# The first FFN unit of a streaming-encoder block, written out in a fixed order with half weight tiles, and the second half of the norm's sum moved among the second unit's products

## The chip, the core and the metric

The kernel runs on one NeuronCore of a Trainium2 chip. The metric is device time in microseconds (us) of one execution, median of several runs. Five engines run their own instruction queues side by side: TensorE (PE: matrix products and transposes, with PEld for its weight loads), VectorE (DVE), ScalarE (ACT), GpSimd (POOL) and SyncE (SP, which here issues most of the transfers from memory). An instruction that waits for another engine holds up everything behind it in its own queue.

## The reference

One layer on a sequence of 512 tokens of width 1024, float32:

```
x = x + 1/2 * SwiGLU(RMSNorm(x))        # FFN 1, inner width 2816
h = RMSNorm(x); p = h @ W_in            # then two token mixers, RWKV-7 and forgetting attention
x = x + (sigmoid(g_A) * y_A + sigmoid(g_B) * y_B) @ W_out
x = x + 1/2 * SwiGLU(RMSNorm(x))        # FFN 2
out = RMSNorm(x)
# SwiGLU(h) = (silu(h @ w1) * (h @ w3)) @ w2
# RMSNorm(x) = x * rsqrt(mean(x*x) + 1e-6) * gain
```

Everything in this document happens in the first lines of FFN 1: loading x, its norm, and the first columns of `h @ w1` and `h @ w3`.

## The kernel before

**Layout.** x is kept transposed, as eight tiles `xT[0..7]` of 128 features x 512 tokens. x arrives in four quarters `xin0..3` (128 x 4 x 256, 512 KB each). PE transposes each quarter into two tiles in PSUM (`xtp`, four transposes a tile), and ACT copies them out to `xT`.

**Float32 products from two parts.** Each operand is split into a high part (rounded to the matrix format) and a low part (the rest): `xh`/`xl` for x times the norm's gain, `firsth`/`firstl` or `whi`/`wlo` for weights. One product of x and w is then three matrix products: high by high, high by low, low by high (`mm3`, lines L130 to L132). The norm's division comes later: products run on x times gain, and the result is multiplied by `rstd` when it leaves PSUM.

**FFN 1** goes in 22 units of 128 columns of w1 and w3. A unit is 2 x 8 x 3 = 48 products of 128x512, one PSUM bank for w1's columns (`f0` in the first unit, `pa` later) and one for w3's (`f1`, `pb`). Its weights come as two tiles of 128x8x128 (512 KB); ACT casts the high part (L122), DVE subtracts for the low part (L123). The loop for units 1 to 21 (second unit on) is in `ffn`; the first unit is written out ahead of it, among the transposes.

**The first unit before.** The transfers go on SP's queue in the order xin0, w1's tile, xin1, w3's tile, xin2, xin3. For each of the eight tiles of x: transposes, copy, high part (on ACT or DVE, by turns), low part on DVE (L182 to L185), then the products whose inputs are there. The order in which the instructions finally stand on each engine is set by a scheduler, which places them by its own estimate of readiness; `tc.keep_in_program_order` pins an instruction at the place where it is written, and `tc.issue_after(i)` puts an instruction behind `i` if both are on the same engine (it makes no engine wait for another). The low part of w3's first tile is cut by POOL.

**The norm.** `nrm.square` squares each tile of x on ACT and adds the squares up (`acc`, the first two additions on POOL, the others on DVE). `nrm.gather` makes the last addition and splits the sum into two halves `shi` (ACT) and `slo` (DVE). `nrm.sums` adds over the 128 partitions on PE, by two products with a matrix of ones (`ssum`, L148): they stand among the products of the second unit. `nrm.root` makes `rstd` of it (ACT); then `evacuate` can empty the first unit's two banks (`fa`, `fb` ...).

**Warm products.** Eight products of a matrix of ones (`warm`, L242) run on PE at the start, before x is there; their result is not used.

Of the kernel before, what the change touches and what calls it, by code (L numbers as in the profile page):

```python
# [18 lines left out]
P = 128  # L19
# [32 lines left out]
def kernel(  # L52
# [73 lines left out]
    def load_w(aps, kt, n, eng=None, own=None):  # L126
        return split_w(load_raw(aps, kt, n), kt, n, eng, own)
# [17 lines left out]

    def summed(ps, mat, parts):
        for i, part in enumerate(parts):
            pe.matmul(ps, mat[:], part[:], start=i == 0, stop=i == 1)  # L148

    def exact(ps, mat, src):  # L150
        summed(ps, mat, halved(src))
# [17 lines left out]
    class Norm:  # L169
# [39 lines left out]

        def sums(s):  # L210
            s.ps = bank("ssum", pr)
            summed(s.ps[:], onesr, s.parts)

        def root(s):
            ln = tmp("rln")
# [29 lines left out]
    dve.tensor_copy(par[:, 0:8], gtp[:, 0:8])  # L245
    nrm = Norm(PAR_FFN1)
    with tc.tile_pool(name="x0", bufs=1) as x0:
        xin = [x0.tile([P, NB, D // 4], F32, name=f"xin{g}") for g in range(4)]
        own = [[x0.tile([P, KD, P], F32R, name=f"first{i}{w}") for i in "hl"] for w in range(2)]
        wraw = [x0.tile([P, KD, P], F32, name=f"wraw{w}") for w in range(2)]  # L250
        first = []
        for g in range(4):
            nc.sync.dma_start(xin[g][:], x[0, :, g * 256:(g + 1) * 256].rearrange("(b p) c -> p b c", p=P))
            for w, at in ((ffn1_w1, 0), (ffn1_w3, 1)):
                if g == at:
                    first.append(load_raw([(0, w[0][:, 0:P])], KD, P, wraw[at]))
        for c in range(KD):
            ps = bank("xtp", pr)
            for b in range(NB):
                pe.transpose(ps[:, b * P:(b + 1) * P], xin[c // 2][:, b, (c % 2) * P:(c % 2 + 1) * P], ident[:])  # L260
            cx = act.copy(xT[c][:], ps[:])
# [4 lines left out]
            for i, at in enumerate((0, 2)):  # L266
                for k in range(KD):
                    if c == max(k, at) if k <= at else c == k:
                        ps, (wh, wl) = first[i]
                        mm3(ps[:], wh[:, k, :], wl[:, k, :], nrm.hi[k][:], nrm.lo[k][:], k == 0, k == KD - 1)  # L270
# [67 lines left out]
    def ffn(nrm, w1, w3, w2, nxt, during=(), first=None, final=None):  # L338
        with tc.tile_pool(name="hp", bufs=1) as hp:
            hh, hl, done = [], [], []  # L340

            def evacuate():
                while done:
                    j, pa, pb = done.pop(0)
                    a = tmp("fa")
                    dve.tensor_tensor(a[:], pa[:], nrm.rstd[:], op=ALU.mult)  # L346
# [12 lines left out]
            for j in range(KF):  # L359
                c0 = j * P  # L360
                early = j == 1 and first
                if j == 0 and first:
                    pa, pb = [f[0] for f in first]
# [707 lines left out]
```

## Time and profile before

| what | before |
|---|---|
| median of 3 runs | 1191.12 us (1190.68 to 1191.21) |
| the profiled execution | 1190.24 us, its span 1188.5 us |
| PE busy | 1169.2 us (98%) |
| DVE / ACT / POOL busy | 662.1 / 457.1 / 100.4 us |
| moved by transfers | 122.54 MB, mean 103 GB/s |
| first product of the second unit (`pa`) | 24.80 us after the span's start |

The span is the time between the first and the last instruction of the profile; the execution's own time has 1.7 us more around it. Busy time of an engine is the sum over its instructions; one engine's idle time costs nothing as long as another carries the end. The granted clock of PE (1.00 is full speed) is given by stretches.

### The profile page before, as it was taken

The page shows a single profiled execution, that of the slowest core. Times are in us where ns is not written, and L with a number is a line of the kernel's source. Part 1 is how long each engine was busy: PE and PEld are TensorE (multiplying, and loading weights), DVE is VectorE, ACT ScalarE, POOL GpSimd, SP SyncE. Part 2 cuts the span into 40 slices and gives each one's busy share as a digit, 9 for nine tenths or more (in the row PEclk, how much of TensorE's full clock was granted, in tenths as well). Part 3 has the DMA queues.
Part 4 walks back from the last instruction along what each step waited for, and adds up shares of the span by engine and source line. Part 5 has one row for each costly group of instructions (what it writes and reads, how often), then busy time and mean ns, then how long its engine had stood idle before and what let it go on. Part 6 is the DMA issues. An engine that isn't in the chain of part 4 may idle for free.

```text
span 1188.5 us, 15870 instructions
## 1 busy us (share of the span) xinstructions
PE 1169.2 (98%) x6334; PEld 952.3 (80%) x6334; DVE 662.1 (56%) x993; ACT 457.1 (38%) x739; POOL 100.4 (8%) x144
## 2 busy tenths in 40 slices
PE   8999999999999999999999999999999999999997
PEld 7888888888887888887767777778888888888887
DVE  6555545443444888686766657866545545543242
ACT  6322222222223855346776756524222222222221
POOL 4200000001111112401000011121000000000110
PEclk9999999999999999999999999999999999999999
DMA  7333333323333433344212135633333333323331
GB/s 200 89 91 104 89 106 89 103 83 115 116 116 96 121 108 111 111 124 116 55 46 87 55 99 175 193 100 107 89 98 98 90 105 91 104 80 98 98 98 72
DMA packets 208152, 122.54 MB, mean 103 GB/s; under 512 B 9902, under 2 KB 200430, under 8 KB 208078
## 3 DMA queue, kind: packets, MB, share of 16 engines
q1 hardware_dynamic: 202078, 108.67, 31.8%
q0 software_dynamic: 3760, 12.06, 3.2%
q8 instruction: 50, 0.82, 0.3%
q10 hardware_dynamic: 2240, 0.79, 0.3%
q14 instruction: 24, 0.20, 0.1%
HBM read 110.82 MB, written 10.68 MB: 102 GB/s over the span
## 4 chain that ended last, share of the span: by engine, by line
PE 95%; DVE 3%; ACT 1%; DMA 1%; issue 0%; POOL 0%; SPq 0%; DVEq 0%; POOLq 0%
PE pd L131 7%; PE pd L130 7%; PE pd L132 7%; PE pa L132 7%; PE pa L131 7%; PE pb L131 7%; PE pb L132 7%; PE pa L130 7%; PE pb L130 7%; PE pgt L130 3%; PE pgt L132 2%; PE pgt L131 2%; PE pk L130 2%; PE pk L132 2%; PE pk L131 2%; PE pw L132 1%
## 5 line engine op out<-in xcount | busy, mean ns | idle before, releaser
L122 ACT CAST whi<-raw 128x1024 fp32r<-128x1024 f32 (+2 forms) x197 | 196.4, 998 | 605.9 <-PE pa L131 175.5
L123 DVE TENSOR_TENSOR wlo<-raw,whi 128x1024 fp32r<-128x1024 f32 (+2 forms) x197 | 227.5, 1155 | 129.1 <-ACT whi L122 129.0
L132 PE MATMUL pa<-xh,wlo 128*128 128x512 f32 x344 | 133.9, 389 | 0.0
L131 PE MATMUL pa<-xl,whi 128*128 128x512 f32 x344 | 133.8, 389 | 0.0
L132 PE MATMUL pb<-xh,wlo 128*128 128x512 f32 x344 | 133.8, 389 | 0.0
L130 PE MATMUL pa<-xh,whi 128*128 128x512 f32 x344 | 133.8, 389 | 0.0
L130 PE MATMUL pb<-xh,whi 128*128 128x512 f32 x344 | 133.8, 389 | 0.0
L131 PE MATMUL pb<-xl,whi 128*128 128x512 f32 x344 | 133.8, 389 | 0.0
L132 PE MATMUL pd<-hh,wlo 128*128 128x512 f32 x330 | 129.0, 391 | 0.0
L131 PE MATMUL pd<-hl,whi 128*128 128x512 f32 x330 | 128.5, 389 | 0.0
L130 PE MATMUL pd<-hh,whi 128*128 128x512 f32 x330 | 128.4, 389 | 0.0
L350 DVE TENSOR_TENSOR fb<-pb,rstd 128x512 f32<-128x512 f32 x43 | 29.7, 691 | 137.2 <-PE pb L132 137.2
L130 PEld LDWEIGHTS pa<-xh,whi 128*128 128x128 f32 x344 | 64.6, 188 | 13.5
L132 PEld LDWEIGHTS pb<-xh,wlo 128*128 128x128 f32 x344 | 64.6, 188 | 13.4
L131 PEld LDWEIGHTS pb<-xl,whi 128*128 128x128 f32 x344 | 64.6, 188 | 13.5
L132 PEld LDWEIGHTS pa<-xh,wlo 128*128 128x128 f32 x344 | 64.5, 188 | 13.5
L131 PEld LDWEIGHTS pa<-xl,whi 128*128 128x128 f32 x344 | 64.6, 188 | 13.4
L130 PEld LDWEIGHTS pb<-xh,whi 128*128 128x128 f32 x344 | 64.5, 188 | 13.4
L131 PEld LDWEIGHTS pd<-hl,whi 128*128 128x128 f32 x330 | 61.9, 188 | 12.9
L132 PEld LDWEIGHTS pd<-hh,wlo 128*128 128x128 f32 x330 | 62.0, 188 | 12.7
L130 PEld LDWEIGHTS pd<-hh,whi 128*128 128x128 f32 x330 | 62.0, 188 | 12.7
L346 DVE TENSOR_TENSOR fa<-pa,rstd 128x512 f32<-128x512 f32 x43 | 29.7, 691 | 68.5 <-PE pa L132 68.4
(397 smaller groups left out, 1964.5 us busy)
## 6 DMA issues: line engine op xcount, KB each, us to landing
raw<-in_ffn_w_dram SPq DMA_DIRECT2D x116, 512.0 KB
raw<-in_w_in_dram SPq DMA_DIRECT2D x40, 512.0 KB
raw<-in_ffn_w_dram SPq DMA_DIRECT2D x15, 384.0 KB
raw<-in_w_out_dram SPq DMA_DIRECT2D x8, 512.0 KB
gsave<-gs SPq DMA_DIRECT2D x9, 256.0 KB
xin<-in_x_dram SPq DMA_DIRECT2D x4, 512.0 KB
xsave<-xT POOLq DMA_DIRECT2D x8, 256.0 KB, 2.3
G<-gsave POOLq DMA_DIRECT2D x8, 256.0 KB, 3.8
```

Source lines behind the costliest of these rows:

```text
L122: act.copy(hi[:], raw[:])
L123: (eng or dve).tensor_tensor(lo[:], raw[:], hi[:].bitcast(F32), op=ALU.subtract)
L130: pe.matmul(ps, whi, xhi, start=first, stop=False)
L131: pe.matmul(ps, whi, xlo, start=False, stop=False)
L132: return pe.matmul(ps, wlo, xhi, start=False, stop=last)
L346: dve.tensor_tensor(a[:], pa[:], nrm.rstd[:], op=ALU.mult)
L350: dve.tensor_tensor(b[:], pb[:], nrm.rstd[:], op=ALU.mult)
```

## The change

The first unit is written out by hand, every instruction pinned in its place (`keep`):

- The weights of the first unit come as four half tiles of 128x4x128 (256 KB each): `w0`, `w1` are the two halves of w1's columns, `w2`, `w3` those of w3's. The transfers' order is x0, w0, x1, w1, x2, x3, w2, w3. Each half has its own cast (`cut(i, False)`, ACT) and subtraction (`cut(i, True)`, DVE).
- Four more warm products follow the transposes of x's first quarter.
- PE makes all products of w1's columns first, each as soon as its tile of x is meant to be ready, with the transposes between them, and then those of w3's; the products of the last tile with w1 stand behind half of w3's.
- ACT makes the high parts of tiles 1, 3, 5, 7, DVE those of 0, 2, 4, 6 and all low parts; POOL has nothing to do in the first unit. All additions of squares are on DVE, behind the last subtraction, and the squares on ACT behind the last cast; the second unit's weights are cut behind these too.
- The second product of the norm's sum (`slo`) stands behind two groups of three products of the second unit's `pb`; before, the scheduler had it further back.

The core of the diff (`turn(c)`: four transposes of tile c; `copy(c)`: `xT[c]` on ACT; `cut(i, lo)`: high or low part of weight half i; `part(c, lo)`: high or low part of tile c of x; `product(w, k, n)`: the n-th of the three products of bank `f0` or `f1` with tile k; the last part is in `ffn`, where `early` is the second unit):

```diff
-        for g in range(4):
-            nc.sync.dma_start(xin[g][:], x[0, :, g * 256:(g + 1) * 256].rearrange("(b p) c -> p b c", p=P))
-            for w, at in ((ffn1_w1, 0), (ffn1_w3, 1)):
-                if g == at:
-                    first.append(load_raw([(0, w[0][:, 0:P])], KD, P, wraw[at]))
-        for c in range(KD):
-            ps = bank("xtp", pr)
-            for b in range(NB):
-                pe.transpose(ps[:, b * P:(b + 1) * P], xin[c // 2][:, b, (c % 2) * P:(c % 2 + 1) * P], ident[:])
-            cx = act.copy(xT[c][:], ps[:])
-            nrm.scale(c, act if (85 >> c) & 1 else dve)
-            for i, at in enumerate((0, 2)):
-                if c == at:
-                    first[i] = (bank(f"f{i}"), split_w(first[i], KD, P, (dve, pool)[i], own[i]))
...
-        with tc.issue_after(cx.ins):
-            for c in range(KD):
-                nrm.square(c, pool if c < 3 else dve)
+        for what in ("x0", "w0", "x1", "w1", "x2", "x3", "w2", "w3"):
+            (load_x if what[0] == "x" else load_first)(int(what[1]))
+        turn(0)
+        turn(1)
+        for _ in range(4):
+            keep(pe.matmul(warm[:, 0:P], ones_[:], ones_[:], start=True, stop=True))
+        copy(0)
+        cut(0, False)
+        copy(1)
+        part(0, False)
+        part(0, True)
+        cut(0, True)
+        part(1, False, act)
+        product(0, 0, 0)
+        product(0, 0, 1)
+        turn(2)
+        turn(3)
+        product(0, 0, 2)
+        part(1, True)
+        for n in range(3):
+            product(0, 1, n)
...
+        for k in range(4):
+            for n in range(3):
+                product(1, k, n)
+        for n in range(3):
+            product(0, 7, n)
+        hi3 = cut(3, False)
+        lo3 = cut(3, True)
+        for k in range(4, KD):
+            for n in range(3):
+                done = product(1, k, n)
+        first.append([i.ins for i in (hi3, lo3, done)])
+        with tc.issue_after(hi3.ins), tc.issue_after(lo3.ins):
+            for c in range(KD):
+                nrm.square(c, dve)
...
+                    gates = []
                     for ps, w in ((pa, w1), (pb, w3)):
-                        mms = nrm.cols(ps[:], *load_w([(0, w[0][:, c0:c0 + P])], KD, P), P)
+                        with ExitStack() as order:
+                            for i in behind if early else ():
+                                order.enter_context(tc.issue_after(i))
+                            mms = nrm.cols(ps[:], *load_w([(0, w[0][:, c0:c0 + P])], KD, P), P, gates)
                         if early and w is w1:
                             with tc.issue_after(mms[-1].ins):
-                                nrm.sums()
+                                total = nrm.sums()
                             nrm.root()
+                            gates = [mms[-1], mms[-1]] + [total] * (KD - 2)
                             evacuate()
```

How the change stands on the engines. On PE, from the second tile of x on (names: `xin1` is x's second quarter, `f0` the bank of w1's columns, `f1` that of w3's; a row with x4 is four instructions). Before:

```order
L260 MATMUL xtp_182<-ident_78,xin1_138 128x128 x4
L260 MATMUL xtp_207<-ident_78,xin1_138 128x128 x4
L130 MATMUL f0_163<-xh0_159,firsth0_141 128x512
L131 MATMUL f0_163<-xl0_160,firsth0_141 128x512
L132 MATMUL f0_163<-xh0_159,firstl0_142 128x512
L130 MATMUL f0_163<-xh1_175,firsth0_141 128x512
L131 MATMUL f0_163<-xl1_176,firsth0_141 128x512
L132 MATMUL f0_163<-xh1_175,firstl0_142 128x512
L260 MATMUL xtp_223<-ident_78,xin2_139 128x128 x4
L260 MATMUL xtp_239<-ident_78,xin2_139 128x128 x4
L130 MATMUL f1_192<-xh0_159,firsth1_143 128x512
```

Now:

```order
L299 MATMUL warm_122<-ones_85 128x128 x4
L294 MATMUL f0_161<-xh0_180,firsth0_141 128x512
L294 MATMUL f0_161<-xl0_181,firsth0_141 128x512
L269 MATMUL xtp_190<-ident_78,xin1_138 128x128 x4
L269 MATMUL xtp_195<-ident_78,xin1_138 128x128 x4
L294 MATMUL f0_161<-xh0_180,firstl0_142 128x512
L294 MATMUL f0_161<-xh1_185,firsth0_141 128x512
L294 MATMUL f0_161<-xl1_186,firsth0_141 128x512
L294 MATMUL f0_161<-xh1_185,firstl0_142 128x512
L294 MATMUL f0_161<-xh2_207,firsth0_141 128x512
L269 MATMUL xtp_214<-ident_78,xin2_139 128x128 x4
```

The warm products and the first two products moved ahead of the second quarter's transposes, and w3's products (`f1`) moved away to the end.

On DVE, from the first tile on (`xh`, `xl`: high and low part of a tile of x; `firstl`: low part of weights). Before:

```order
L123 TENSOR_TENSOR firstl0_142<-wraw0_145,firsth0_141 128x1024
L184 TENSOR_SCALAR xh1_175<-xT1_112,par_119 128x512
L185 SCALAR_TENSOR_TENSOR xl0_160<-xT0_111,par_119,xh0_159 128x512
L185 SCALAR_TENSOR_TENSOR xl1_176<-xT1_112,par_119,xh1_175 128x512
L184 TENSOR_SCALAR xh3_213<-xT3_114,par_119 128x512
L185 SCALAR_TENSOR_TENSOR xl3_214<-xT3_114,par_119,xh3_213 128x512
```

Now:

```order
L283 TENSOR_SCALAR xh0_180<-xT0_111,par_119 128x512
L279 SCALAR_TENSOR_TENSOR xl0_181<-xT0_111,par_119,xh0_180 128x512
L288 TENSOR_TENSOR firstl0_142<-wraw0_149,firsth0_141 128x512
L279 SCALAR_TENSOR_TENSOR xl1_186<-xT1_112,par_119,xh1_185 128x512
L283 TENSOR_SCALAR xh2_207<-xT2_113,par_119 128x512
L279 SCALAR_TENSOR_TENSOR xl2_208<-xT2_113,par_119,xh2_207 128x512
L288 TENSOR_TENSOR firstl1_144<-wraw1_150,firsth1_143 128x512
L279 SCALAR_TENSOR_TENSOR xl3_227<-xT3_114,par_119,xh3_226 128x512
```

x's first tile now goes ahead of the weights' low part, which has half the width, and the tiles go strictly in order.

On PE again, in the second unit, from the norm's first sum on (`shi`, `slo`: the halves of the sum of squares). Before, the second sum stood behind eleven products of `pb`, the last of them

```order
L131 MATMUL pb_327<-xl2_189,whi_380 128x512
L132 MATMUL pb_327<-xh2_188,wlo_381 128x512
L130 MATMUL pb_327<-xh3_213,whi_380 128x512
L131 MATMUL pb_327<-xl3_214,whi_380 128x512
L148 MATMUL ssum_358<-slo_323,onesr_87 128x512
```

and now behind six:

```order
L148 MATMUL ssum_374<-shi_338,onesr_87 128x512
L130 MATMUL pb_343<-xh0_180,whi_396 128x512
L131 MATMUL pb_343<-xl0_181,whi_396 128x512
L132 MATMUL pb_343<-xh0_180,wlo_397 128x512
L130 MATMUL pb_343<-xh1_185,whi_396 128x512
L131 MATMUL pb_343<-xl1_186,whi_396 128x512
L132 MATMUL pb_343<-xh1_185,wlo_397 128x512
L148 MATMUL ssum_374<-slo_339,onesr_87 128x512
```

The second sum moved five products ahead. From the third unit on the order is the one before on every engine, but for a few neighbours on DVE and POOL that change places.

More of the change, by code (lines that the diff above doesn't have):

```diff
@@ L147, in summed @@
         for i, part in enumerate(parts):
-            pe.matmul(ps, mat[:], part[:], start=i == 0, stop=i == 1)
+            mm = pe.matmul(ps, mat[:], part[:], start=i == 0, stop=i == 1)
+        return mm
     def exact(ps, mat, src):
@@ L211, in sums @@
             s.ps = bank("ssum", pr)
-            summed(s.ps[:], onesr, s.parts)
+            return summed(s.ps[:], onesr, s.parts)
         def root(s):
@@ L247 @@
     with tc.tile_pool(name="x0", bufs=1) as x0:
+        keep = tc.keep_in_program_order
         xin = [x0.tile([P, NB, D // 4], F32, name=f"xin{g}") for g in range(4)]
-        own = [[x0.tile([P, KD, P], F32R, name=f"first{i}{w}") for i in "hl"] for w in range(2)]
-        wraw = [x0.tile([P, KD, P], F32, name=f"wraw{w}") for w in range(2)]
-        first = []
-        for g in range(4):
-            nc.sync.dma_start(xin[g][:], x[0, :, g * 256:(g + 1) * 256].rearrange("(b p) c -> p b c", p=P))
-            for w, at in ((ffn1_w1, 0), (ffn1_w3, 1)):
-                if g == at:
-                    first.append(load_raw([(0, w[0][:, 0:P])], KD, P, wraw[at]))
@@ L271, with load_x, load_first @@
-        with tc.issue_after(cx.ins):
+        own = [[x0.tile([P, 4, P], F32R, name=f"first{i}{w}") for i in "hl"] for w in range(4)]
+        wraw = [x0.tile([P, 4, P], F32, name=f"wraw{w}") for w in range(4)]
+        def load_x(g):
+            keep(nc.sync.dma_start(xin[g][:], x[0, :, g * 256:(g + 1) * 256].rearrange("(b p) c -> p b c", p=P)))
+        def load_first(i):
+            k0 = i % 2 * 4
+            load_raw([(0, (ffn1_w1, ffn1_w3)[i // 2][0][k0 * P:(k0 + 4) * P, 0:P])], 4, P, wraw[i])
@@ new lines, with turn, copy @@
+        for what in ("x0", "w0", "x1", "w1", "x2", "x3", "w2", "w3"):
+            (load_x if what[0] == "x" else load_first)(int(what[1]))
+        first = [bank(f"f{i}") for i in range(2)]
+        xtps = [None] * KD
+        def turn(c):
+            xtps[c] = bank("xtp", pr)
+            for b in range(NB):
+                keep(pe.transpose(xtps[c][:, b * P:(b + 1) * P], xin[c // 2][:, b, (c % 2) * P:(c % 2 + 1) * P], ident[:]))
+        def copy(c):
+            keep(act.copy(xT[c][:], xtps[c][:]))
@@ new lines, in part @@
+        def part(c, lo, eng=dve):
+            if not lo:
+                nrm.hi[c], nrm.lo[c] = [xp.tile([P, T], F32R, tag=f"x{i}{c}", name=f"x{i}{c}") for i in "hl"]
+            hi, g = nrm.hi[c], pc(nrm.gain + c)
+            if lo:
+                keep(dve.scalar_tensor_tensor(nrm.lo[c][:], xT[c][:], g, hi[:].bitcast(F32), op0=ALU.mult, op1=ALU.subtract))
+            elif eng is act:
+                keep(act.activation(hi[:], xT[c][:], AF.Copy, scale=g))
+            else:
+                keep(dve.tensor_scalar(hi[:], xT[c][:], g, None, op0=ALU.mult))
@@ new lines, in cut, with product @@
+        def cut(i, lo):
+            hi_, lo_ = own[i]
+            if lo:
+                return keep(dve.tensor_tensor(lo_[:], wraw[i][:], hi_[:].bitcast(F32), op=ALU.subtract))
+            return keep(act.copy(hi_[:], wraw[i][:]))
+        def product(w, k, n):
+            wt = own[2 * w + k // 4][n // 2][:, k % 4, :]
+            x_ = (nrm.hi[k], nrm.lo[k], nrm.hi[k])[n]
+            return keep(pe.matmul(first[w][:], wt, x_[:], start=k == 0 and n == 0, stop=k == KD - 1 and n == 2))
+        turn(0)
@@ new lines @@
+        turn(1)
[16 more added lines that the diff above has]
+            product(0, 1, n)
+        copy(2)
+        copy(3)
@@ new lines @@
+        part(2, False)
+        part(2, True)
+        cut(1, False)
+        cut(1, True)
+        product(0, 2, 0)
+        turn(4)
+        product(0, 2, 1)
+        product(0, 2, 2)
+        turn(5)
+        part(3, False, act)
+        part(3, True)
+        for n in range(3):
+            product(0, 3, n)
+        copy(4)
+        copy(5)
+        part(4, False)
+        part(4, True)
+        product(0, 4, 0)
+        turn(6)
+        turn(7)
+        product(0, 4, 1)
+        product(0, 4, 2)
@@ new lines @@
+        part(5, False, act)
+        part(5, True)
+        for n in range(3):
+            product(0, 5, n)
+        copy(6)
+        copy(7)
+        part(6, False)
+        part(6, True)
+        for n in range(3):
+            product(0, 6, n)
+        cut(2, False)
+        part(7, False, act)
+        cut(2, True)
+        part(7, True)
+        for k in range(4):
+            for n in range(3):
+                product(1, k, n)
+        for n in range(3):
+            product(0, 7, n)
+        hi3 = cut(3, False)
@@ L362, in ffn @@
                 if j == 0 and first:
-                    pa, pb = [f[0] for f in first]
+                    pa, pb, behind = first
                 else:
```

6 lines of the change are left out of this document (1 added, 5 removed).

## The prediction

> **What bounds the kernel now.** I read the page first, then the start of TensorE's timeline, then the busy time by stretches, then ACT, DVE, POOL and the DMA queue in the same microseconds. The page gives the span, TensorE's (PE's) busy time and the chain of work that ended last:
>
> ```profile
> span 1188.5 us, 15870 instructions
> PE 1169.2 (98%) x6334; PEld 952.3 (80%) x6334; DVE 662.1 (56%) x993; ACT 457.1 (38%) x739; POOL 100.4 (8%) x144
> PE 95%; DVE 3%; ACT 1%; DMA 1%; issue 0%; POOL 0%; SPq 0%; DVEq 0%; POOLq 0%
> ```
>
> TensorE is the bound everywhere: a microsecond is won only where PE stands still or runs slowly. The change touches the first two units of the first FFN, so I read PE's timeline there (columns: start, duration, engine, line, operation, count; in brackets the idle time before).
>
> ```profile
> 1.14 3.78 PE L242 MATMUL warm<-ones 128*128 128x128 f32 x16 [1.14 <-DVE ones L84]
> 5.05 1.97 PE L260 MATMUL xtp<-ident,xin 128*128 128x128 f32 x8
> 9.57 1.12 PE L260 MATMUL xtp<-ident,xin 128*128 128x128 f32 x8 [2.55 <-DVE firstl L123]
> ...
> 11.77 0.63 PE L130 MATMUL f<-xh,firsth 128*128 128x512 f32 x1
> 12.20 0.63 PE L131 MATMUL f<-xl,firsth 128*128 128x512 f32 x1
> ...
> 15.04 1.03 PE L260 MATMUL xtp<-ident,xin 128*128 128x128 f32 x8
> 15.83 0.48 PE L131 MATMUL f<-xl,firsth 128*128 128x512 f32 x1
> ...
> 24.57 0.39 PE L132 MATMUL f<-xh,firstl 128*128 128x512 f32 x1
> 24.80 0.39 PE L130 MATMUL pa<-xh,whi 128*128 128x512 f32 x1
> ```
>
> Three things are to be seen. PE is idle for 2.55 us before 9.57. The named releaser is a DVE operation, but the transposes there read the second quarter of x, so its transfer fits as well. A product costs 0.43 us around 12 us (11.77 to 12.20) and 0.23 later (24.57 to 24.80). The second unit (tile pa) starts at 24.80. In the list of PE's waits the next ones after the 2.6 us here lie in the mixers' stages, hundreds of microseconds later, such as this one,
>
> ```profile
> PE xtp L260 <- DVE firstl L123: 2.6, 1, 2.6
> PE ppj L130 <- ACT whi L122: 1.6, 1, 1.6
> ```
>
> so **the time of pa's first product is what the change can move**. The clock column says why the products were slow:
>
> ```profile
> 1.14:3.62 2.48, 2.48 (x11) 2.48 (x12) 1.17 (x9) 1.28 (x1) 0.30 (x2) 1.00 0.61 184
> 3.62:7.03 3.41, 3.40 (x16) 2.75 (x14) 0.17 (x1) 0.00 (x0) 0.00 (x0) 1.00 0.98 288
> 7.03:10.45 3.42, 0.88 (x9) 0.91 (x9) 2.21 (x3) 2.85 (x5) 0.00 (x0) 1.00 1.11 322
> 10.45:13.86 3.41, 3.41 (x12) 2.74 (x11) 2.98 (x5) 2.45 (x4) 1.50 (x1) 0.50 1.13 325
> 13.86:16.00 2.14, 2.14 (x18) 1.95 (x17) 2.10 (x3) 1.91 (x4) 0.99 (x1) 1.00 1.16 291
> ```
>
> (Stretch, length, then busy us of PE, PEld, DVE, ACT, POOL, then granted clock, DMA share, GB/s.) From 7.03 to 10.45 PE was busy 0.88 of 3.42 us; in the 3.41 us behind that the granted clock was 0.50, after 3.41 us of work 1.00 again. Half a clock over 3.41 us is 1.7 us of lost work. The floor without idling and without the halved clock: 48 products x 0.23 = 11.0, 24 transposes at 0.1 (eight from 15.04 to 15.83) = 2.4, in all 13.4 us.
>
> **The change, part by part.**
>
> *Four warm matmuls behind the first eight transposes.* In the first row 16 passes take 3.78 us, 0.236 each, two to a matmul; the transposes at 5.05 (1.97 for eight, against 0.79 later) show PE slow until about 7. Eight passes cost 1.9 us at that pace and 0.9 at twice it; they begin at 7.02, so I take 0.9: they end at 7.95, inside the idle 2.55 us, at no cost.
>
> *Half weight tiles, loaded between the quarters of x.* A quarter of x and an old weight tile are 512 KB each, a new one 256 KB. Summing GB/s over the stretches (0.46 MB by 3.62, 1.44 by 7.03, 2.54 by 10.45, 3.65 by 13.86), the second quarter of x, the third transfer, had its 1.57 MB moved at 7.4 and was used at 9.57, 2.1 later; the weights' cast below began 1.5 after their 1.05 MB (5.7). I take a lag of 1.5 to 2.1. In the new order this quarter ends at 1.31 MB: 6.6 + 2.1 = **8.7**; the third at 2.10 MB, 10.6 to 11.2; the fourth at 2.62, 12.2 to 12.8; the last weight half at 3.15 MB, 13.8 to 14.4. SP issues two transfers more, hidden: its rows wait inside the issue for room,
>
> ```profile
> 3.65 4.14 SPq L253 DMA_DIRECT2D xin<-in_x_dram  x2
> 7.83 6.10 SPq L110 DMA_DIRECT2D raw<-in_ffn_w_dram  x3
> ```
>
> and the next unit's weights still end at 3.67 MB.
>
> *ACT and DVE, in written order.* The prices:
>
> ```profile
> 7.17 1.04 ACT L122 CAST firsth<-wraw 128x1024 fp32r<-128x1024 f32 x1 [4.41 <-DMA wraw<-in_ffn_w_dram]
> 8.12 1.06 ACT L261 COPY xT<-xtp 128x512 f32<-128x512 f32 x2
> 9.07 0.74 ACT L182 ACTIVATE xh<-xT,par 128x512 fp32r<-128x512 f32 x1
> 17.16 1.68 ACT L195 ACTIVATE sq<-xT 128x512 f32<-128x512 f32 x3
> 20.92 1.28 ACT L135 ACT_TABLE_LOAD   x1
> 28.06 0.62 ACT L142 CAST shi<-acc 128x512 fp32r<-128x512 f32 x1 [3.22 <-DVE acc L207]
> ```
>
> ```profile
> 8.24 1.23 DVE L123 TENSOR_TENSOR firstl<-wraw,firsth 128x1024 fp32r<-128x1024 f32 x1 [2.92 <-ACT firsth L122]
> 9.39 0.48 DVE L184 TENSOR_SCALAR xh<-xT,par 128x512 fp32r<-128x512 f32 x1
> 9.84 1.42 DVE L185 SCALAR_TENSOR_TENSOR xl<-xT,par,xh 128x512 fp32r<-128x512 f32 x2
> ...
> 12.93 2.47 DVE L185 SCALAR_TENSOR_TENSOR xl<-xT,par,xh 128x512 fp32r<-128x512 f32 x1 [0.30 <-ACT xh L182]
> ...
> 21.42 0.69 DVE L197 TENSOR_TENSOR acc<-acc,sq 128x512 f32<-128x512 f32 x1 [1.19 <-POOL acc L197]
> ```
>
> ```profile
> 12.36 2.49 POOL L123 TENSOR_TENSOR firstl<-wraw,firsth 128x1024 fp32r<-128x1024 f32 x1 [10.87 <-ACT firsth L122]
> 17.88 3.51 POOL L197 TENSOR_TENSOR acc<-acc,sq 128x512 f32<-128x512 f32 x2 [3.03 <-ACT sq L195]
> ```
>
> One low part of x took 2.47 us instead of 0.71, exactly while POOL cut the second weight's low part (12.36 to 14.85). The change gives that cut and POOL's two additions to DVE, so in this stretch POOL is empty. I take 0.71 for every low part; the 2.47 stays as a rival.
>
> DVE now paces the unit. ACT copies the first transposed tile as soon as it is there (half of 1.97 after 5.05, some 0.3 to finish: 6.3 to 6.9), no longer behind the cast at 7.17. DVE's first high part starts at 6.95. Up to the low part of tile 6, DVE owes 4 high parts x 0.48, 7 low x 0.71 and 2 weight halves x 0.65 (between 1.23/2 and 0.69): 1.9 + 5.0 + 1.3 = 8.2, so 15.15 without waits. Waits: tile 2 is transposed at 8.7 + 0.4, finished 0.2 later and copied in 0.6, at 9.9, while DVE is free at 9.5: 0.4. Tile 5, behind the third quarter, costs 0.2 to 0.4 in the same way. So tile 6's low part is ready at about 15.8, and PE then owes 2 + 27 products x 0.23 = 6.6: **pa starts at 22.4**. By PE alone it is 7.95 + 13.4 = 21.35. If the second quarter of x came no earlier than 9.57, all of it moves by 0.87, and the spread of the lag (0.6) may come on top for the others: 23.9. I take 22.4, since DVE's row is the nearest limit: **gain 24.80 - 22.4 = 2.4 us**, with ends 0.9 and 3.45.
>
> *Unit two must keep up.* ACT owes 8 copies x 0.53, 4 casts x 0.62 and 4 high parts x 0.74 from 6.3 on, 9.7 us, and with the waits for x ends its last weight cast near 16.8. Five squares (0.56 each) and the cast of pa's weights (1.05) end at 20.7, needed at 22.4. The low part (1.23) ends at 21.9, needed at 22.85. Then table load, second cast, three squares: 24.7; on DVE the low part of pb's weights and three additions: 26.3. The halved sum is ready at 27.0 (high) and 27.7 (low). PE reaches the norm's first sum at 22.4 + 24 x 0.23 = 27.9, and the second, now fixed six products later, at 29.5. The spare is 0.9 and 1.8 us, so I cost this part at nothing; each microsecond beyond the spare is paid in full, since PE's products queue behind the sum.
>
> ```profile
> 32.99 0.39 PE L148 MATMUL ssum<-slo,onesr 128*128 128x512 f32 x1
> 36.19 0.39 PE L130 MATMUL pa<-xh,whi 128*128 128x512 f32 x1
> ```
>
> ```profile
> 34.87 0.69 DVE L346 TENSOR_TENSOR fa<-f,rstd 128x512 f32<-128x512 f32 x1 [2.30 <-ACT rstd L218]
> ```
>
> Before, the second sum stood 8.2 us behind pa's start, now 7.1, so the evacuation that frees the first bank for unit three (34.87, needed at 36.19) gets 1.1 us more room. From unit three on, each engine's order is the one before but for a few neighbours on DVE: nothing later gives the gain back.
>
> *Sum.* The profiled execution took 1190.24 (span 1188.5) and would take 1187.8. It lies 0.88 below the median of the three runs shown, so against that median: 1191.12 - 2.4 = **1188.7**. About 0.2% (2.4 us) is what a measurement of this kernel can tell from no change, and my gain stands on that edge.
>
> **A rule weighed.** PE's transposes fill much of the gap that the change closes, so it matters whether they hold the clock up. In the rows, 3.62 to 7.03 held 1.3 us of warm matmuls and 1.97 of transposes, and PE came out of it fast (the transposes at 9.57 run at the later pace), whereas 1.14 to 3.62, 2.48 us of warm matmuls, had left it slow. [...]
>
> **Rivals.**
> - *The clock halves again* (1190.1). Between 7.03 and 10.45 the new order leaves PE 0.9 us of warm matmuls, about 1.4 of products and 0.8 of transposes. If 3.1 of 3.4 us (2.3 without the transposes) is too little, the next 3.41 us run at 0.50: 1.7 us, of which DVE's pace hides up to 0.6, so a gain of 0.7 to 1.3. For it: 2.48 us of 3.4 did not raise the clock at first. Against: holding is not raising, and 0.88 was what dropped it. [...]
> - *x comes no earlier* (1189.6). If the 2.1 us lag is not bytes in the queue, the second quarter again starts at 9.57, 0.87 later, and the gain is 1.55. Against: the queue moved 290 to 325 GB/s without a break.
> - *The norm is late* (1190 to 1191): the sum's high half over 0.9 us late. ACT's stretch from 16.8 to 24.7 has no room, which speaks for it.
> - *Slower, 1194*: the 2.47 us low part is not POOL's doing but strikes DVE by itself. Each costs 1.76, and in written order PE's products stand behind every one. One leaves a gain of 0.6, two lose; three (5.3 - 2.4 = 2.9 slower) decide. Against: its neighbours at 9.84 took 0.71, and the long one ends 0.55 after POOL's cut. [...]
>
> **How the numbers follow.** The forecast has 0.66 (own range 1187.7 to 1189.5, 0.46 of it beyond 0.2%), and 0.02 lies below that. The halved clock has 0.12, x no earlier 0.10, the norm late 0.04, all within 0.2%; the slow low parts have 0.06, slower. Hence faster 0.48, same 0.46, slower 0.06. The range takes in the forecast, the first two rivals and 0.4 us for the spread of runs: 1187.3 to 1190.8.
>
> **What would show it.** Right: the second quarter's transposes near 8.7; a clock of 1.00 from about 7 on; no low part over 0.8 us; pa's first product near 22.4; no PE wait at ssum; 2.4 us between pa's start and the same point before, kept to the end. Wrong: a stretch at 0.50 behind 10 us, PE waiting on xl from DVE for over 1 us in all, or pa waiting for its cast on ACT.

## The result, and the profile after

| | before | after |
|---|---|---|
| median, 14 runs each on one chip | 1190.72 us (1189.08 to 1192.48) | 1187.53 us (1186.93 to 1189.37) |
| ratio to before, 95% interval | | 0.9977 (0.9969 to 0.9985) |
| the same on a second chip (27 and 10 runs) | 1190.73 us | 1188.21 us, 0.9977 (0.9967 to 0.9986) |
| the profiled execution (span) | 1190.24 us (1188.5) | 1188.99 us (1187.2) |
| first product of `pa` | 24.80 | 22.30 |
| first product of unit three | 36.19 | 33.69 |

The change is faster by 0.23%: 2.5 to 3.2 us between medians. The timeline of PE in the profile of after has the columns start, duration, engine, line, operation and tiles, and in brackets the idle time ahead with what ended it:

```profile
6.30 1.06 PE L299 MATMUL warm<-ones 128*128 128x128 f32 x8
8.35 1.03 PE L269 MATMUL xtp<-ident,xin 128*128 128x128 f32 x8
10.48 0.60 PE L269 MATMUL xtp<-ident,xin 128*128 128x128 f32 x4
15.59 0.50 PE L294 MATMUL f<-xl,firsth 128*128 128x512 f32 x1 [0.17 <-DVE xl L279]
22.30 0.39 PE L130 MATMUL pa<-xh,whi 128*128 128x512 f32 x1
27.74 0.39 PE L148 MATMUL ssum<-shi,onesr 128*128 128x512 f32 x1
29.35 0.39 PE L148 MATMUL ssum<-slo,onesr 128*128 128x512 f32 x1
33.69 0.39 PE L130 MATMUL pa<-xh,whi 128*128 128x512 f32 x1
```

`pa` starts 2.50 us earlier and unit three too: nothing of it is given back in unit two. The waits of PE between 5 and 34 us (what waited, for whom, us in total, times, longest) are down to one line, where the old order had one wait of 2.55 us:

```profile
PE f L294 <- DVE xl L279: 0.4, 2, 0.2
```

DVE's groups from 5 to 18 us (busy, mean ns) hold eight low parts of x at a mean of 750 ns, with no long one among them:

```profile
L279 DVE SCALAR_TENSOR_TENSOR xl<-xT,par,xh 128x512 fp32r<-128x512 f32 x8 | 6.0, 750 | 0.3 <-ACT xh L281 0.2
L288 DVE TENSOR_TENSOR firstl<-wraw,firsth 128x512 fp32r<-128x512 f32 x4 | 2.7, 684 | 0.0
```

DVE's timeline has its first high part of x and the low part of tile 6, behind which PE takes up the product at 15.59:

```profile
6.68 0.49 DVE L283 TENSOR_SCALAR xh<-xT,par 128x512 fp32r<-128x512 f32 x1 [1.36 <-ACT xT L272]
14.78 0.75 DVE L279 SCALAR_TENSOR_TENSOR xl<-xT,par,xh 128x512 fp32r<-128x512 f32 x1
```

Yet the span of the profiled execution fell only by 1.3. The rest is lost at 610 us, in code that the change does not touch: the same PE products come 2.51 us earlier than before at 605 us and 1.04 us earlier at 625, and 1.19 at the end. Work by stretches (after the bounds in us and the length: PE's busy time, PEld, DVE, ACT, POOL, then PE's granted clock, the share of the DMA engines and GB/s), and PE's waits there:

```profile
5.74:9.16 3.42, 3.20 (x25) 2.69 (x24) 2.44 (x4) 2.49 (x5) 0.00 (x0) 1.00 1.08 337
606.48:609.90 3.42, 1.50 (x9) 0.88 (x7) 3.26 (x8) 2.40 (x6) 0.00 (x0) 1.00 0.00 0
609.90:613.31 3.41, 3.40 (x14) 2.33 (x14) 2.83 (x7) 1.38 (x7) 0.00 (x0) 0.50 0.01 2
```

```profile
PE lp L960 <- ACT qrn L817: 1.2, 1, 1.2
PE ups L886 <- DVE Xs L882: 0.8, 1, 0.8
```

The first row is the start of the kernel: 3.20 us of work where before had 0.88, and the clock stays at 1.00. The other two are the two mixers: a stretch with 1.50 us of work, and behind it one at half clock. Before's profile has the same two waits, but its stretches are cut at other places there: 607.77 to 611.19 held 2.24 us of work and 611.19 to 614.60 held 2.64, and the clock stayed at 1.00. So the two profiles alone would have the gain (1190.24 to 1188.99, 1.25 us) at half its size or less.

**Reading the runs by their clock.** Each run beside the experiments, and each of the changed kernel, lists its mean granted clock. A stretch of 3.41 us at half clock takes 0.5 x 3.41 / 1187 = 0.0014 off it, and the last 3 to 4 us of every trace, where PE runs out of work at half clock, take 0.0013 to 0.0017. So 0.998 or 0.999 means no other such stretch, 0.997 one, 0.996 or less two or more. The fourteen traces bear this out: seven show no such stretch (0.998 or 0.999), five show one (0.997), two show two (0.996, e7 and e11). All runs that list a clock, over the chips, with the median of each group in brackets:

| kernel | runs | median | none | one | two or more |
|---|---|---|---|---|---|
| before | 75 | 1190.75 | 3 (1189.34) | 21 (1189.83) | 51 (1191.00) |
| after | 24 | 1187.74 | 17 (1187.52) | 7 (1189.07) | 0 |

By after's groups a stretch costs about 1189.07 - 1187.52 = 1.55 us, by before's 1191.00 - 1189.83 = 1.17. Before had at least (21 + 2 x 51)/75 = 1.64 of them in a run, after 7/24 = 0.29: an estimate of 1.6 to 2.1 us of the 3.0 between these medians. The profiled execution of before, with one stretch, was better than its median run.

### The profile page after: what moved, and what is told of

Read it like the earlier page. It is cut to its first block, busy times and chain, and to the rows that moved or that the text cites. A ratio compares the mean times of both kernels' runs of the same rounds, so it can differ in the third digit from the quotient of the medians.

```text
span 1187.2 us, 15895 instructions
## 1 busy us (share of the span) xinstructions
PE 1170.3 (99%) x6342; PEld 953.1 (80%) x6342; DVE 664.4 (56%) x998; ACT 457.7 (39%) x741; POOL 94.0 (8%) x141
## 4 chain that ended last, share of the span: by engine, by line
PE 95%; DVE 3%; ACT 1%; issue 0%; DVEq 0%
PE pd L130 7%; PE pd L132 7%; PE pd L131 7%; PE pa L130 7%; PE pb L130 7%; PE pb L132 7%; PE pa L132 7%; PE pa L131 7%; PE pb L131 7%; PE pgt L130 3%; PE pgt L132 2%; PE pgt L131 2%; PE pk L130 2%; PE pk L132 2%; PE pk L131 2%; PE pw L132 1%
```

## The experiments

e1 to e4 ran together on one chip, e5 to e8 on another; e9 to e11 are one execution each, and e12 repeats e6.

### The two sources apart: warm products and the order of the transfers

Without the four warm products:

```
-        for _ in range(4):
-            keep(pe.matmul(warm[:, 0:P], ones_[:], ones_[:], start=True, stop=True))
```

> The changed kernel without its four warm matmuls between the first two transposed tiles and the first product; nothing else is altered. Theory (they only fill idle time, and the order itself keeps PE busy enough): the clock stays at 1.00 behind 10 us, pa's first product stays at 22.3 (22.1 to 22.5), the median stays within 0.3 us of the changed kernel's. Rival (the clock is what the change bought, and the warm matmuls hold it): without them PE has about 1.06 us less work between 6.3 and 8.0, a stretch of 3.41 us at 0.50 appears between 8 and 14 us, and pa starts at 23.5 to 24.0, median +1.2 to +1.7 us.

With the old order of bytes ahead of x's quarters:

```
-  for what in ("x0", "w0", "x1", "w1", "x2", "x3", "w2", "w3"):
+  for what in ("x0", "w0", "w1", "x1", "w2", "w3", "x2", "x3"):
```

> The changed kernel with its transfers in the order x0, w0, w1, x1, w2, w3, x2, x3: the same bytes ahead of every quarter of x as in the kernel before, nothing else altered. Theory (x's quarters are placed by the bytes ahead of them, and the transfer order brought part of the gain): the second quarter's transposes move from 8.35 back to 9.4 to 9.7, the third's from 10.48 to about 12, and pa starts 0.9 to 1.5 us later, at 23.2 to 23.8; the clock stays at 1.00 because of the warm matmuls; median +0.9 to +1.5 us. Rival (it is the clock alone): the quarters come later, but the clock stays at 1.00 and PE catches up from its own slack, so pa stays at 22.3 to 22.6. Second rival (the gap opens again and the clock halves in spite of the warm matmuls): pa at 24.5 to 25, as before, median +2 to +2.7 us.

And both edits together:

> Both of the two edits: the late order of transfers and no warm matmuls, so that the written order and the half weights alone remain of the change. Clock theory: PE has only some 2 us of work between 7 and 10.5 us, the clock halves for 3.41 us as it did before, and pa starts at 24.5 to 25.0, that is 1 to 1.7 us behind the late order with warm matmuls; median +2.2 to +2.7 us, about the kernel before. Rival (the order of the products and the half weights brought the gain by themselves): pa at 23.2 to 23.8, no stretch at 0.50, no more than the late order alone.

| (11 runs each, before 1190.88) | median | ratio to before | none / one / two or more stretches at half clock |
|---|---|---|---|
| e1, no warm products | 1189.63 | 0.9992 (0.9983 to 1.0001) | 4 / 3 / 4 |
| e2, late x | 1190.20 | 0.9996 (0.9987 to 1.0005) | 5 / 6 / 0 |
| e3, late x and no warm products | 1191.39 | 1.0000 (0.9991 to 1.0009) | 3 / 1 / 7 |

What is left of the change in e3, the written order and the half tiles, brings nothing by itself that these runs can tell: the ratio is 1.0000, within 0.09%. Either source alone brings 0.04 to 0.08%, within the interval of nothing; together they are worth 0.23%. That this is more than the sum of the two is not shown, since each interval is 0.09% wide to either side.

The traces tell how. PE of e1:

```profile
6.88 0.47 PE L294 MATMUL f<-xh,firsth 128*128 128x512 f32 x1 [0.85 <-DVE xh L283]
22.55 0.39 PE L130 MATMUL pa<-xh,whi 128*128 128x512 f32 x1
```

The place of the warm products is an idle time of 0.85 us, and `pa` starts at 22.55: as work they cost and bring next to nothing, as the theory said. But its execution was one without a stretch at half clock; 7 of 11 had one or more, against 7 of 24 with the warm products, and 4 of 11 had two or more, against none of 24. The median is nearer to what the rival expected (1.4 to 2.1 us behind the changed kernel's, 1.2 to 1.7 expected). PE of e2 (three rows), and below it that of e3 (two):

```profile
9.73 1.09 PE L269 MATMUL xtp<-ident,xin 128*128 128x128 f32 x8 [1.49 <-DMA xin<-in_x_dram]
13.11 0.63 PE L269 MATMUL xtp<-ident,xin 128*128 128x128 f32 x4 [1.02 <-DMA xin<-in_x_dram]
24.75 0.39 PE L130 MATMUL pa<-xh,whi 128*128 128x512 f32 x1
```

```profile
8.01 1.08 PE L269 MATMUL xtp<-ident,xin 128*128 128x128 f32 x8
23.06 0.39 PE L130 MATMUL pa<-xh,whi 128*128 128x512 f32 x1
```

In e2 the second quarter comes 1.4 us later than in the profile of after, the third 2.6, and `pa` starts 2.45 later, at full clock (this trace's one stretch at half clock comes at 612.8 us, behind 1.48 us of work): more than the 0.9 to 1.5 of the theory, because PE waits twice for x (2.5 us) and cannot use the time between. In e3, with the same order, x's second quarter was there at 8.01, and the trace looks as the rival had it, with `pa` at 23.06 and no stretch at half clock, while the median of the eleven runs is about that of before, as the theory had it. The arrival differs by 1.7 us between two executions with the same queue: in the slice from 5 to 6 us the queue moved 229 GB/s in e2's trace and 306 in e3's.

One more execution of each, to catch the stretch:

> The changed kernel without its four warm matmuls, a second look, since 7 of its 11 runs showed a granted clock of 0.997 or 0.996 and the one with the trace did not. Theory (the warm matmuls hold the clock in some positions of the stretches only): with 0.996 or 0.997 the trace shows a stretch at half clock between 4 and 14 us, and ahead of it a stretch with less than 1.75 us of PE work; pa at 23.2 to 24.5. Rival (what they cost is work for the clock at about 608 us alone): no stretch at half clock before 600 us, pa at 22.2 to 22.9. With 0.998 it tells neither apart.

> The late order of transfers without the warm matmuls, a second look, since 7 of its 11 runs showed 0.996 and the one with the trace 0.998. Theory (the gap ahead of the second quarter of x, with no warm matmuls in it, drops the clock in most positions of the stretches): one or two stretches at half clock between 7 and 15 us, pa at 24.5 to 26.5. Rival (x is early in this execution too): second quarter's transposes at about 8, no stretch at half clock, pa near 23.

e10 took 1188.45 us at 0.998, so it tells neither apart, as the expectation says. Its least stretch at the start held 2.19 us of PE work, 0.35 above the most that has been followed by a drop of the clock in any trace (1.84, below). Cut anywhere else, no stretch at the start of this trace or of e1's would hold less than 2.18. So the stretches at half clock that the kernel's runs show more often are not seen in place. That they lie at the start is only inferred, and would need executions in which x comes later than in these two. e11 took 1192.75 us and shows them; PE first, then the work by stretches:

```profile
10.07 1.19 PE L269 MATMUL xtp<-ident,xin 128*128 128x128 f32 x8 [2.26 <-DMA xin<-in_x_dram]
25.50 0.39 PE L130 MATMUL pa<-xh,whi 128*128 128x512 f32 x1
```

```profile
7.50:10.91 3.41, 1.15 (x9) 0.84 (x10) 1.03 (x2) 0.36 (x2) 0.00 (x0) 1.00 1.10 322
10.91:14.32 3.41, 3.39 (x13) 2.42 (x12) 2.50 (x4) 2.12 (x4) 0.00 (x0) 0.50 1.14 314
751.60:755.01 3.41, 1.84 (x7) 0.97 (x6) 1.90 (x4) 3.39 (x6) 0.00 (x0) 1.00 1.04 377
755.01:758.43 3.42, 3.42 (x10) 2.70 (x9) 2.61 (x5) 2.30 (x4) 0.00 (x0) 0.50 0.52 159
```

Late x and no warm products leave 1.15 us of work between 7.50 and 10.91, and the clock halves, as in the profile of before: the theory's outcome. The second stretch at half clock of this run lies at 755 us, which neither theory had.

### POOL beside DVE

The second half tile's low part is cut by POOL:

```
-  return keep(dve.tensor_tensor(lo_[:], ...
+  return keep((pool if i == 1 else dve).tensor_tensor(lo_[:], ...
```

> The changed kernel with the low part of the second half of the first weight cut by POOL instead of DVE. Theory (DVE's two-input operations from SBUF wait out a POOL operation that reads SBUF): POOL's cut takes about 1.3 us, and the low part of x that stands beside it on DVE takes 1.3 to 2.5 us instead of 0.74; DVE gains 0.65 and loses about 1 to 1.7, so pa starts 0.3 to 1.2 us later than 22.3, median +0.3 to +1.2 us. Rival (the 2.47 us low part of before was DVE's own, by chance or from the transfers): all low parts stay at 0.74, DVE is relieved of 0.65 us, pa starts at 21.7 to 22.3, median 0 to -0.5 us.

Measured: 1188.61 us, ratio 0.9983 (0.9974 to 0.9992); among the runs without a stretch at half clock 1188.3, against 1187.5 of the changed kernel. POOL's cut, and two low parts on DVE, one beside it and one later:

```profile
10.63 1.36 POOL L288 TENSOR_TENSOR firstl<-wraw,firsth 128x512 fp32r<-128x512 f32 x1 [9.14 <-ACT firsth L289]
```

```profile
11.20 1.33 DVE L279 SCALAR_TENSOR_TENSOR xl<-xT,par,xh 128x512 fp32r<-128x512 f32 x1 [0.35 <-ACT xh L281]
15.17 0.75 DVE L279 SCALAR_TENSOR_TENSOR xl<-xT,par,xh 128x512 fp32r<-128x512 f32 x1
```

The low part beside POOL takes 1.33 instead of 0.75 and ends 0.54 us behind POOL, as the 2.47 us one of before did (0.56). The theory holds; `pa` starts at 22.68, so the price is small. And from the other side, the kernel before with POOL's cut and its two additions on DVE:

```
-  first[i] = (bank(f"f{i}"), split_w(first[i], KD, P, (dve, pool)[i], own[i]))
+  first[i] = (bank(f"f{i}"), split_w(first[i], KD, P, (dve, dve)[i], own[i]))
-  nrm.square(c, pool if c < 3 else dve)
+  nrm.square(c, dve)
```

> The kernel before, with the second weight's low part and the three additions of squares that POOL did given to DVE; written order, transfers and tile sizes of before. Theory (POOL's cut lengthened DVE's low part of x to 2.47 us, but that lay behind the late transfer of x and the halved clock, so it cost little): every low part of x at 0.71 to 0.75, pa starts at 24.0 to 24.8, median 0 to -0.8 us. Rival (POOL's contention was a main term of the gain): pa starts at 22.9 to 23.8, median -1 to -2 us. Second rival (DVE, which now owes 1.2 us more for the cut and 1.4 for the additions, becomes the bound): pa at 25 or later, median +0.3 to +1.5 us.

Measured: 1190.90 us, ratio 1.0001 (0.9992 to 1.0010). DVE's group of low parts, then PE:

```profile
L185 DVE SCALAR_TENSOR_TENSOR xl<-xT,par,xh 128x512 fp32r<-128x512 f32 x8 | 5.8, 748 | 0.2
```

```profile
9.43 1.07 PE L260 MATMUL xtp<-ident,xin 128*128 128x128 f32 x8 [2.41 <-DMA xin<-in_x_dram]
24.66 0.39 PE L130 MATMUL pa<-xh,whi 128*128 128x512 f32 x1
```

The 2.47 us low part is gone and nothing is won: it lay behind the late x and the halved clock. So in the old order freeing POOL is no term of the gain; in the new one, where DVE sets the pace, one cut left to POOL cost 0.4 us of `pa`'s start in e4. The wait at 9.43 is put down to the DMA of x here; in the profile of before the same idle time bore the name of DVE's `firstl`.

### The second unit's order

The changed kernel again as the measure, and it without `behind` and the gates of the sum:

```
-  for i in behind if early else ():
+  for i in ():
-  gates = [mms[-1], mms[-1]] + [total] * (KD - 2)
+  gates = []
```

> The changed kernel itself, unaltered, as the measure for the runs beside it on the same chip. Both theories of the clock: the runs fall into two groups about 1.6 us apart, near 1187.4 (mean granted clock 0.998 to 0.999) and near 1189.1 (0.997), with about one run in three in the second; none with 0.996 or less. Median 1187.3 to 1188.2; pa starts at 22.2 to 22.7.

> The changed kernel without the two edits to the second unit: its first products are no longer issued behind the first unit's last, and the second half of the norm's sum has no fixed place. In the program's order 21 of pa's products then stand ahead of the first unit's last 28, and both weight casts of the second unit come earlier on ACT. Theory (PE has no more work than before, but is made to wait for a weight that comes last from memory): pa's first product comes at 17 to 18.5 instead of 22.3, PE waits 1 to 3 us ahead of it on the cast of pa's weights, and the third unit starts 1 to 3 us later than 33.7; median +1 to +3 us. Rival (the order is free: every product is needed anyhow, and pa's weights have landed by then): the third unit starts at 33.5 to 34.0 and the median is within 0.4 us.

e5: 1188.21 us, seven of ten runs with no stretch at half clock, three with one. `pa` started at 22.82 in its trace, a little behind the 22.2 to 22.7 expected; PE waited 0.58 us for x's second quarter, until 8.72. e7: 1193.75 us, ratio 1.0020 (1.0011 to 1.0029). PE of e7, and its stretches:

```profile
16.54 0.50 PE L130 MATMUL pa<-xh,whi 128*128 128x512 f32 x1 [1.63 <-ACT whi L122]
17.80 0.50 PE L132 MATMUL pa<-xh,wlo 128*128 128x512 f32 x1 [0.52 <-DVE wlo L123]
38.52 0.50 PE L130 MATMUL pa<-xh,whi 128*128 128x512 f32 x1 [1.07 <-DVE fa L439]
```

```profile
14.89:18.31 3.42, 1.26 (x5) 0.77 (x5) 1.23 (x1) 2.84 (x4) 0.00 (x0) 1.00 1.00 248
18.31:21.72 3.41, 3.41 (x9) 2.66 (x9) 3.20 (x5) 3.41 (x7) 0.00 (x0) 0.50 0.04 9
```

Against e5 the loss is 5.5 us, where the expectation had 1 to 3 and only the wait for the cast. Unit three starts at 38.52, 4.83 later than 33.69; this is 1.63 + 0.52 of waits, 1.7 of a stretch at half clock that these waits bring about, and 1.07 because the norm is late and the first bank is not free: 4.9. This trace has a second stretch at half clock at 615.7 us, behind 1.60 us of work. So the fixed order of the second unit, which the prediction costed at nothing, keeps the rest from being lost; the two edits were taken away together, and their shares are not told apart.

### Filling the wait at 608 us

Five more products, whose result is overwritten, ahead of the first product of `lp` in the second pass; nothing else is altered:

```
   lps.append(lp)
+  for _ in range(5 if p == 1 and i == 0 and q == 0 else 0):
+      pe.matmul(lp[:], onesr[:], mix.hi[0][:], start=True, stop=True)
```

> The changed kernel with five more products of 128x512, whose result is overwritten, ahead of the first product of lp in the second pass of the attention part, where PE otherwise waits 1.2 us for ACT at about 608 us; nothing else is altered. Theory (the second group of runs comes from one stretch of 3.41 us behind this wait, in which the clock is halved because the stretch before held only 1.5 us of PE work): the five products (5 x 0.23 = 1.1 us) lift that stretch to 2.6 us, no run shows 0.997, all lie at 1186.9 to 1187.8, and the median falls by 0 to 0.6 us against the changed kernel. Rival (the second group has another cause, or the products do not reach the threshold): two groups as before, median as the changed kernel's or up to 0.3 us more, since lp then waits for the last of the five.

> The changed kernel with the five products in the wait at 608 us, again, for more runs of it. Over all places of a stretch of 3.41 us between 600 and 612 us the least PE work is 1.47 us in the changed kernel's trace and 2.63 us with the five products; 1.2 of 3.41 us of the positions lie below 1.75 us in the changed kernel. Theory: the changed kernel falls into the slower group in 1.2/3.41 = 35% of its runs (so far 7 or 8 of 24), this one in none of 11; median 1187.2 to 1187.7. Rival (the 6 runs without one were chance): three or four of 11 runs at 0.997 and 1188.9 or more.

e6: 1187.50 us over 6 runs, 0.9969 (0.9956 to 0.9981); e12: 1187.56 over 11 runs, 0.9979 (0.9970 to 0.9988). PE at the place, and the stretch behind it:

```profile
607.21 1.44 PE L958 MATMUL lp<-xh,onesr 128*128 128x512 f32 x5
608.49 0.22 PE L962 MATMUL lp<-kb,qa 128*128 128x128 f32 x1
```

```profile
606.50:609.91 3.41, 2.76 (x15) 1.87 (x13) 3.29 (x7) 2.38 (x5) 0.00 (x0) 1.00 0.00 0
608.52:611.93 3.41, 2.63 (x21) 1.92 (x20) 3.29 (x8) 1.84 (x7) 0.00 (x0) 1.00 0.00 0
```

The work there is lifted as meant: no place of a stretch between 600 and 612 us holds less than 2.6 us. Of the 17 runs two had a stretch at half clock, against 7 of 24 without the fill, and e12's "none of 11" was wrong by these two. Such a difference may be chance, and the medians (1187.5 against 1187.5 and 1188.2) lie within each other's spread: a gain over the changed kernel is not shown. A candidate for the two runs is the place at 750 us, which halved the clock in e11 behind 1.84 us of work; e12's own trace has 1.83 there and kept the clock:

```profile
749.95:753.36 3.41, 1.83 (x8) 1.31 (x8) 3.01 (x5) 2.57 (x6) 0.00 (x0) 1.00 0.65 240
```

### The kernel before, a second execution

> The kernel before, unaltered, to see a run of its commonest kind: a mean granted clock of 0.996, where its profile showed 0.997. So far every stretch of 3.41 us that held up to 1.68 us of PE work was followed by one at half clock, and none that held 1.82 us or more; and a stretch with 2.66 us of work did not raise it at the start. Theory of the stretches: a mean of 0.996 is two stretches at half clock in a row behind the gap ahead of the second quarter of x, because the first of them still holds part of the gap and so too little work to raise the clock; pa then starts at 25.0 to 26.0. Rival: the second stretch at half clock is the one behind the wait at about 609 us, and pa starts at 24.4 to 24.9. If the run shows 0.997, one stretch only, it tells neither apart.

It took 1190.10 us at 0.997, so it does not tell the theories of 0.996 apart; where the second stretch of most of before's runs lies stays open. But it shows the kernel before with x early by chance:

```profile
8.60 1.07 PE L260 MATMUL xtp<-ident,xin 128*128 128x128 f32 x8 [1.66 <-DMA xin<-in_x_dram]
23.47 0.39 PE L130 MATMUL pa<-xh,whi 128*128 128x512 f32 x1
```

```profile
6.70:10.12 3.42, 1.76 (x12) 1.31 (x11) 2.74 (x4) 3.10 (x6) 0.00 (x0) 1.00 1.12 326
607.44:610.86 3.42, 1.72 (x10) 1.06 (x8) 3.26 (x8) 2.37 (x6) 0.00 (x0) 1.00 0.00 0
```

1.76 us of work at the start held the clock, `pa` came at 23.47 instead of 24.80, and the clock halved behind the 1.72 us at 610 instead. This trace has three long low parts on DVE: 2.35 us beside POOL's cut, 1.67 and 1.78 beside POOL's two additions, which the prediction did not count. Its `pa` is still the earliest of the three traces of the old order, which fits e8.

## Why the prediction was right, and where it was not

- **The start of `pa`.** 22.4 was worked out from DVE's debt, 22.30 came, and on the way that was forecast: DVE began at 6.68 (6.95 forecast), tile 6's low part was ready at 15.53 (15.8), and from 15.59 on 29 products of 0.23 us stood ahead of `pa`. That the profile meets the number to 0.1 us is luck in part, since it is the earliest of its kind. Over the seven traces with the new transfers and the fixed second unit it lies between 22.30 and 23.11, mean 22.65; the three traces with the order of before (24.80, 24.66 in e8, 23.47 in e9) have a mean of 24.31. The single pair of profiles gives 2.5, the means 1.7. All three traces of the old order are of executions at 0.997, the smaller group; the 51 of 75 at 0.996 or less were not seen in a trace, and with them the difference may be larger.
- **x comes earlier.** 8.7 was expected for the second quarter. Eight traces with the new order have 7.94 to 8.99, mean 8.42; the six with the old order of bytes 8.01 to 10.07, mean 9.24. Bytes in the queue set the mean, 0.8 us, and single executions lie up to 1.2 us to either side; the prediction had a spread of 0.6.
- **The warm products cost nothing.** Right as work. But the step counted nothing for them on the other side either, and e1 puts 1.4 to 2.1 us of the median on them. They were to be judged with the rival of the halved clock, not by the idle time that they fill: without them more runs have stretches at half clock, which e11 shows at the start for the late order and no trace shows for the early one.
- **The clock.** The first rival did not come true in any of the five traces that have the warm products and the early x: no stretch at 0.50 at the start, unless e7's order makes one.
- **No long low part, POOL's doing.** Eight of 0.75 us; e4 brings a long one back at will, e8 takes it away from before. The rival by which DVE itself is slow is ruled out. That it was worth nothing by itself, e8 adds.
- **The norm in time.** The first sum at 27.74 and the second at 29.35, forecast at 27.9 and 29.5, with no wait.
- **The size.** 1188.7 was forecast and 1187.53 came. 0.4 of the difference is the base (1190.72 in these runs, 1191.12 in the three shown). The rest is the step from the profiled execution of 1190.24 to one of 1187.8: it took 1188.99, while most other runs took less. The mis-sized term is the clock outside the first 14 us: the sum counted the one stretch at half clock of before's profile, and took none for granted elsewhere. Most runs of before have two or more, and 7 of 24 of after have one, in the profile at a place that the change doesn't touch.
- **The rule weighed.** The sentence that stretches with transposes raised the clock stands: 3.62 to 7.03 of before, with 1.97 us of them, did, and the like stretches of e8 and e9. In the profile of after it rose behind a stretch from 2.33 to 5.74 in which only 0.69 us are transposes of x, so it adds little. The stretches at half clock are 3.413 us long (10.45 to 13.86 in before, 609.90 to 613.31 in after), and each execution has another cut. The clock fell behind stretches in which PE was not idle throughout: they held 0.88 to 1.72 us of work.

## What to carry to other kernels

Before trusting the difference of two profiles to a microsecond, look at the mean granted clock of all runs: in these traces a wait that left PE 0.88 to 1.72 us of work in a stretch of 3.41 was followed by one at half clock, and by after's groups such a stretch costs about 1.55 us, in the share of executions whose stretches are cut that way. Look for such waits over the whole kernel and bridge them, by earlier bytes and by filler products together; here either alone brought a third of the gain or less, which the runs could not tell from nothing, and the filler at 608 us lifted the work without a gain that the runs could show. And when products are moved forward, keep the next unit's behind those whose weights land first.

## What the runs showed of the hardware

- Over 14 traces, eight stretches of 3.413 us with 0.88 to 1.72 us of PE work (the run-out at the end left aside) were all followed by one at half clock. Of fifteen with 1.76 to 1.85, one was (1.84, e11); none with more. At the start, 2.15 to 2.61 us of work had not raised it (before, e8, e9), as the first quarter's transposes show, which took 1.89 to 1.97 us there and 1.09 to 1.45 in the others; 2.95 us had (e11).
- In the changed kernel's trace 1.2 us out of the 3.41 us of possible cuts between 600 and 612 us hold less than 1.75 us: 35%, and 7 of 24 runs had a stretch at half clock. That the cuts are spread evenly over the executions is not shown: the three traces with slow first transposes are the three of the old code.
- The second quarter of x, with the same bytes ahead of it, is used between 8.01 and 10.07 us.
- Five low parts on DVE (two tiles read from SBUF) in the first 25 us that began in the course of a cut or an addition on POOL took 1.33 to 2.47 us instead of 0.75, and each ended 0.54 to 0.56 us behind POOL (before, e4, e9). One more, begun 0.11 us ahead of the end of POOL's addition, took 0.75 (before). Later in before twelve more took 1.78 to 1.79 us beside POOL's additions of 1.50 to 1.96. Not drawn out were `rlo` (L155), of two tiles, beside a memset on POOL (0.68 us at 460.60), `gs` (L545), one of whose two inputs lies in PSUM, beside a copy on POOL (0.68 us at 488.00), both in before, and a high part, of one tile, beside POOL's selects (0.47 us at 12.46, e4).
- SP's first three issues of 512 KB took 0.43 to 0.58 us each, the fourth 1.13, and the next two 2.07 each (before). That they wait for room is the prediction's reading; the rows name no cause.
